# The first expert layer of a two-block network: activation halves side by side in one 512-column matmul, added after the bank is full

## The chip, the cores and the metric

The kernel runs on one core of one Trainium2 chip. The metric is the device time of one launch in microseconds. Five engines work side by side, each through its own list of instructions in a fixed order: TensorE (PE) multiplies matrices into PSUM, VectorE (DVE) and ScalarE (ACT) do the elementwise work, GpSimd (POOL) does almost nothing here, and SyncE (SP) issues the DMAs. An instruction that waits holds up everything behind it on its engine.

## The reference, cut to what matters

256 tokens of width 1024 pass through a first block (a recurrent and an attention branch, a gated feed-forward layer) and then through two layers of a second block. Each layer of the second block ends in a layer of 16384 small experts, which the reference computes only for the chosen ones:

```python
q = (xt @ w_q).reshape(T, PEER_HEADS, 2, PEER_HALF)
s = jnp.einsum('thpe,pne->thpn', q, sub_keys)
top_s, top_i = lax.top_k(s, PEER_TOPK)          # 16 of 128, for two key halves of 8 heads
...
best_s, best_j = lax.top_k(cand, PEER_TOPK)     # 16 of the 256 pairs
expert = idx_a * PEER_N_KEYS + idx_b
gate = jax.nn.softmax(best_s, axis=-1)
...
h = jnp.einsum('td,thkd->thk', xb, u[eb])
a = jax.nn.gelu(h, approximate=False) * gb
return jnp.einsum('thk,thkd->td', a, v[eb])
```

The kernel computes `h` for all experts (256 tokens by 16384 experts), multiplies by a gate matrix that is zero where an expert was not chosen, and multiplies by all of `v`. The result is the same sum.

## The kernel before

**Split products.** Every float32 operand of a large product is split in two parts in the rounded type F32R: `hi` is the rounded value (a cast on ACT, L225) and `lo` the rest (a subtraction on DVE, L226). A product is then three matmuls: high weight by high activation, high weight by low activation, low weight by high activation (`mm3`, L264 to L266; `step_a`, L281 to L283).

**Weights.** `weight` loads a tile of 128 by 2048 values by DMA and splits it in two halves of 1024 columns, so one half costs one `hi` cast and one `lo` subtraction. There are four buffers of split halves (`WBUFS`): the cast of a half waits until the TensorE is done with the half four places earlier. The preparation is put ahead in the program's priorities by 350 instructions (`AHEAD`).

**Expert layer (`peer`, run twice).** The first product works on pairs: `u_pair(j)` takes one weight tile, two blocks of 128 experts by 256 tokens. `proj_b` computes both blocks into one PSUM bank of 512 columns (256 for each block, tag `st`, two banks). Each of the 8 slices of 128 input values takes three matmuls of 256 columns, so a block is 24 matmuls and a pair 48. One Gelu on ACT (L1228) reads the bank and writes the ring `H`, which holds 40 pairs.

**Stages of an expert layer.** (1) Query products and scores; then DVE starts on `top16` (MAX8, FIND_INDEX8, MATCH_REPLACE8), the choice of the experts. (2) 24 pairs of `u` on TensorE, beside which DVE finishes the choice (`select`, `pick`, `gate`, `lookup`; the list `todo`), and `turn` transposes its results. (3) 16 further pairs of `u`, each with about one `gates` step, in which DVE builds one-hot matrices (L1239 to L1242), TensorE multiplies them (L1249, L1250) and DVE multiplies the gates into `H` (L1257). (4) 24 pairs of `u` in turn with `v_pair`, which multiplies `H` by a tile of `v` in 24 matmuls of 512 columns. (5) The rest of `v`.

**Order.** A list scheduler sets the order of each engine's instructions once, when the program is built, from the program's order and the priorities. The chip keeps to it.

Of the kernel before, what the change touches and what calls it, by code (L numbers as in the profile page):

```python
# [10 lines left out]
F32R = mybir.dt.float32r  # L11
F16 = mybir.dt.float16
U32 = mybir.dt.uint32
AF = mybir.ActivationFunctionType
ALU = mybir.AluOpType
# [3 lines left out]
S, D = 256, 1024  # L19
# [7 lines left out]
ALPHA = 4.0 ** 0.25  # L27
G_SCALE = 2048.0

PARTS = (48, 48, 32)  # second keys of the experts that are gated together  # L30
RING = 80  # second keys whose hidden values are on chip at a time
RATE = 0.96  # groups of 16 tokens gated for each tile of expert weights
AHEAD = 350  # instructions by which the weights' preparation runs ahead
WBUFS = 4  # split halves of weight tiles on chip
LEAD = 2  # tiles of the first block left when its attention is through
PACE = 2  # tiles of expert weights to a step of the selection
TURN = 17  # the tile after which the first half's indices are transposed
# memory keys and values of a layer, computed where norms leave the tensor engine free
FILL = ((), ("k1",), ("v1",), (), ("k0", "v0"))
URGENT = 1500  # instructions by which norms go before other work  # L40


def _btiles(w, cols):
# [121 lines left out]
def urgent(f):  # L165
    def run(self, *a, **k):
        with self.tc.high_priority(offset=URGENT):
            return f(self, *a, **k)
# [3 lines left out]
class Net:  # L172
    def __init__(self, ctx, tc, io, out):
# [3 lines left out]
        self.cp = pool("consts", 1)  # L177
        self.wp = pool("weights", WBUFS)
        self.xp = pool("state", 1)
# [36 lines left out]
    def vecs(self, *aps):  # L216
        with self.tc.high_priority(offset=AHEAD):
            t = self.wp.tile([128, 2048], F32, name="raw", tag="raw", bufs=3)
            out = [t[:, j * D:j * D + D] for j in range(len(aps))]
            for o, ap in zip(out, aps):  # L220
                self.nc.sync.dma_start(o, bass.AP(tensor=ap.tensor, offset=ap.offset, ap=[[0, 128], [1, D]]))
        return out
# [11 lines left out]
    def weight(self, src, parts=2):  # L234
        n = src.shape[-1] // parts
        out = []
        with self.tc.high_priority(offset=AHEAD):
            raw = self.raw(src)
# [5 lines left out]
        return out  # L244

    def new_xT(self, nk=8):
        hi = self.xp.tile([128, 8, S], F32R, name="xTh", tag="xTh")
        lo = self.xp.tile([128, 8, S], F32R, name="xTl", tag="xTl")
        return hi, lo

    def to_T(self, dst, src, tt, nk=8, k0=0):
        nc = self.nc
# [15 lines left out]
    def proj_b(self, w, xT, m=128):  # L268
        ps = self.st()
        for n, (hi, lo) in enumerate(w):  # L270
            hi, lo = (t.rearrange("p (k c) -> p k c", c=m) for t in (hi, lo))
            nk = hi.shape[1]
            for k in range(nk):
                self.mm3(ps[:m, n * 256:(n + 1) * 256], hi[:, k], lo[:, k], xT[0][:, k, :], xT[1][:, k, :],
                         k == 0, k == nk - 1)
        return ps

    def step_a(self, ps, w, c, xT, k, t, first, last):
        mm = self.nc.tensor.matmul
        xh, xl = xT[0][:, k, t], xT[1][:, k, t]  # L280
        mm(ps, xh, w[0][:, c], start=first, stop=False)  # L281
        mm(ps, xh, w[1][:, c], start=False, stop=False)  # L282
        mm(ps, xl, w[0][:, c], start=False, stop=last)  # L283
# [47 lines left out]
        return self.sp.tile([128, n], F32, name=name, tag=f"{name}{n}")  # L331

    def table(self, func):
        """Has the table of func loaded behind the scalar engine's work so far."""
        t = self.col("warm")
        self.tc.keep_in_program_order(self.nc.scalar.activation(t, self.eps6, func))

# [56 lines left out]
    def layer_norm(self, acc, gb, xT=None, out=None):  # L394
# [3 lines left out]
        for tt in range(2):  # L398
# [14 lines left out]
            for nh in range(2):  # L413
# [6 lines left out]
                    nc.sync.dma_start(out[tt * 128:tt * 128 + 128, c], x[:, c])  # L420
                if xT is not None:
                    self.to_T(xT, x[:, c], tt, nk=4, k0=4 * nh)
# [1 line left out]
    def load_mem(self):  # L424
        self.memT = tuple(self.mp.tile([128, 8, S], F32R, name=f"memT{s}") for s in "hl")
        raw = self.raw(self.io["memT"].rearrange("p k t -> p (k t)")).rearrange("p (k t) -> p k t", k=8)
        self.split(*self.memT, raw)
        self.km = [self.kp.tile([128, 2, S], F32, name=f"km{l}") for l in range(2)]
        self.vm = [self.kp.tile([128, 2, S], F32, name=f"vm{l}") for l in range(2)]
# [118 lines left out]
    def first_mix(self):  # L548
# [176 lines left out]
        for n, (name, j, f) in enumerate(tiles):  # L725
            f(j, self.proj_b(self.weight(io[name][j]), xT))
            while done < len(units) and done * (len(tiles) - LEAD) < (n + 1) * len(units):
                unit(*units[done])
# [90 lines left out]
    def ple_gate(self, acc, bv, xT):  # L819
        nc = self.nc  # L820
        for tt in range(2):
            h = self.vp.tile([128, D], F32, name="hn", tag="hn")
            for nh in range(2):
# [3 lines left out]
                nc.vector.tensor_mul(h[:, c], h[:, c], self.pproj[:, tt, c])  # L827
                nc.vector.tensor_add(self.x[:, tt, c], self.x[:, tt, c], h[:, c])
                self.to_T(xT, self.x[:, tt, c], tt, nk=4, k0=4 * nh)
# [1 line left out]
    def mem_attn(self, qm, km, vm):  # L831
        nc, pp = self.nc, self.pp
        mP = {}
# [266 lines left out]
    def peer(self, l, xT):  # L1100
        nc, io, pp = self.nc, self.io, self.pp
        two = lambda ps: ps.rearrange("p (a b) -> p a b", a=2)
# [4 lines left out]
        idx = [pp.tile([128, S], F16, name=f"pidx{j}") for j in range(4)]  # L1107
        H = pp.tile([128, RING, S], F32, name="H")
        tk = ExitStack()
# [113 lines left out]
        latest = [None]  # L1223

        def u_pair(j):
            ps = self.proj_b(self.weight(io["u"][l][j]), xT)
            s = (2 * j) % RING
            latest[0] = nc.scalar.activation(H[:, s:s + 2, :], two(ps), AF.Gelu)  # L1228

        def gates(part, t0):  # L1230
            b0, nb = sum(PARTS[:part]), PARTS[part]
            oa = op.tile([128, 4, P_KEYS, 4], F16, name="oa", tag="oa", bufs=2)
            ob, oh, ol = (op.tile([128, 4, max(PARTS), 4], F16, name=n, tag=n, bufs=k)[:, :, :nb]
                          for n, k in (("ob", 1), ("oh", 2), ("ol", 2)))
            c = slice(t0, t0 + 16)
            col = lambda j, n: idx[j][:, c].rearrange("p (g t) -> p g t", t=4)[:, :, None, :].to_broadcast(
                [128, 4, n, 4])
            iot = lambda n0, n: iota[:, None, n0:n0 + n, :].to_broadcast([128, 4, n, 4])
            nc.vector.tensor_tensor(out=oa, in0=iot(0, P_KEYS), in1=col(0, P_KEYS), op=ALU.is_equal)  # L1239
            nc.vector.tensor_tensor(out=ob, in0=iot(b0, nb), in1=col(1, nb), op=ALU.is_equal)  # L1240
            nc.vector.tensor_tensor(out=oh, in0=ob, in1=col(2, nb), op=ALU.mult)
            nc.vector.tensor_tensor(out=ol, in0=ob, in1=col(3, nb), op=ALU.mult)  # L1242
            nt = 16 if nb <= 32 else 8
            for e in range(16 // nt):
                ps = self.ms()
                for n in range(nt):
                    t = e * nt + n
                    o = ps[:, n * nb:n * nb + nb]
                    nc.tensor.matmul(o, oa[:, t // 4, :, t % 4], oh[:, t // 4, :, t % 4], start=True, stop=False)  # L1249
                    nc.tensor.matmul(o, oa[:, t // 4, :, t % 4], ol[:, t // 4, :, t % 4], start=False, stop=True)  # L1250
                g = ps[:, :nt * nb].rearrange("p (t b) -> p b t", t=nt)
                done = 0
                while done < nb:
                    s = (b0 + done) % RING
                    n = min(nb - done, RING - s)
                    h = H[:, s:s + n, t0 + e * nt:t0 + e * nt + nt]
                    nc.vector.scalar_tensor_tensor(h, g[:, done:done + n], 1.0 / G_SCALE, h, op0=ALU.mult,  # L1257
                                                   op1=ALU.mult)
                    done += n
# [3 lines left out]
        def v_prep(j):  # L1263
            s = (2 * j) % RING
            ah = op.tile([128, 2, S], F32R, name="ah", tag="ah", bufs=2)
# [33 lines left out]
        for tt in range(2):  # L1299
            todo += [lambda tt=tt: pick(tt, 0, 4), lambda tt=tt: pick(tt, 4, 4), lambda tt=tt: gate(tt),  # L1300
                     lambda tt=tt: lookup(tt)]
        n0 = PARTS[0] // 2
        for j in range(n0):
            u_pair(j)
            while todo and (10 - len(todo)) * PACE <= j:
                todo.pop(0)()
            if j == TURN:
                turn(0)
# [5 lines left out]
        op = ok.enter_context(self.tc.tile_pool(reuse_waits="tile", name="onehot", bufs=1))  # L1314
        ends = [sum(PARTS[:k + 1]) // 2 for k in range(len(PARTS))]
        queue = [(k, t0) for k in range(len(PARTS)) for t0 in range(0, S, 16)]
        up, vp, due, turn_v = n0, 0, 0.0, True
        while vp < 62:
            low = ends[queue[0][0] - 1] if queue and queue[0][0] else (0 if queue else 64)
            can_u = up < 64 and 2 * up + 2 <= 2 * vp + RING  # L1320
            can_v = vp < low
# [4 lines left out]
            elif can_u:  # L1326
                u_pair(up)
                up += 1
                turn_v = True
            due = min(due + RATE, 2.0) if queue else 0.0  # L1330
            while queue and up >= ends[queue[0][0]] and (due > 0.99 or not (can_u or can_v)):
# [84 lines left out]
```

## Time and profile before

| | |
|---|---|
| time, median of 3 runs (lowest, highest) | 2532.6 us (2531.86, 2533.39) |
| span of the profiled execution | 2531.2 us |
| PE busy | 2497.7 us, 99% |
| DVE busy | 1733.8 us, 68% |
| ACT busy | 1194.2 us, 47% |
| TensorE clock granted, mean | 0.994 of full speed |

The span runs from the first to the last instruction of one profiled execution; the times of the runs hold what lies around it too, here 1.4 us at the median. The first expert layer begins at about 700 us of the span, the second at about 1700 us. A busy TensorE is one with a matmul in flight, so the distance between the starts of two matmuls tells more of its rate than the duration of one.

### The profile page before, as it was taken

To read this page: it belongs to the slowest core of one execution; us is meant where nothing else is said; L and a number is where in the kernel's file an instruction comes from. 1 tells how busy PE (TensorE), PEld (TensorE's weight loads), DVE (VectorE), ACT (ScalarE), POOL (GpSimd) and SP (SyncE) were. 2 spreads that over 40 slices of the span, in tenths; PEclk is the share of its full clock that TensorE was granted. 3 is DMA by queue.
4 is the path that set the end of the run, shared out by engine and by line. 5 is a ranking of instruction groups with operands and counts; after the bars stand their busy time and mean duration, and the time that the engine had idled before them with its cause. 6 is when DMAs were issued, how large, how long until landed. Compare 5 with 4: busy or idle time off the path is not lost.

```text
span 2531.2 us, 44590 instructions
## 1 busy us (share of the span) xinstructions
PE 2497.7 (99%) x18560; PEld 2276.9 (90%) x18560; DVE 1733.8 (68%) x3195; ACT 1194.2 (47%) x1697; POOL 5.9 (0%) x17
## 2 busy tenths in 40 slices
PE   8999999999999999999999999999999999999998
PEld 7998899988799999999988888989999999998887
DVE  5357665565699587588478556669968758748756
ACT  5357554455545533433443445644643443344443
POOL 0000000000000000000000000000000000000000
PEclk9989999999999999999999999999999999999999
DMA  8422455543444544544544554344553454454454
GB/s 295 150 96 92 140 209 190 183 173 109 154 170 167 195 142 148 191 157 143 191 167 156 194 195 158 140 175 165 183 179 139 161 189 143 158 183 167 166 187 147
DMA packets 64410, 420.80 MB, mean 166 GB/s; under 512 B 7520, under 2 KB 10480, under 8 KB 15824
## 3 DMA queue, kind: packets, MB, share of 16 engines
q1 hardware_dynamic: 64208, 417.96, 47.4%
q8 instruction: 145, 2.38, 0.4%
q14 instruction: 57, 0.47, 0.1%
HBM read 416.88 MB, written 1.05 MB: 165 GB/s over the span
## 4 chain that ended last, share of the span: by engine, by line
PE 94%; DVE 3%; ACT 1%; DMA 1%; issue 1%; SPq 0%; DVEq 0%; ACTq 0%
PE ps_st L264 15%; PE ps_st L266 15%; PE ps_st L265 15%; PE ps_acc L281 12%; PE ps_acc L283 12%; PE ps_acc L282 12%; PE ps_ms L1249 3%; PE ps_ms L1250 3%; PE ps_sc L621 1%; PE ps_acc L640 1%; DVE lo L226 1%; ACT hi L225 1%; PE ps_acc L1152 1%; PE ps_sc L494 1%; PE ps_ms L1053 0%
## 5 line engine op out<-in xcount | busy, mean ns | idle before, releaser
L226 DVE TENSOR_TENSOR lo<-raw,hi 128x1024 fp32r<-128x1024 f32 (+1 forms) x762 | 922.8, 1214 | 508.5 <-ACT hi L225 505.5
L225 ACT CAST hi<-raw 128x1024 fp32r<-128x1024 f32 (+1 forms) x762 | 792.8, 1043 | 939.7 <-PE ps_st L265 610.1
L264 PE MATMUL ps_st<-xTh,hi 128*128 128x256 f32 (+1 forms) x3232 | 924.0, 286 | 0.9 <-DVE shift_v L573 0.7
L266 PE MATMUL ps_st<-xTh,lo 128*128 128x256 f32 (+1 forms) x3232 | 919.0, 284 | 0.5 <-DVE lo L226 0.5
L265 PE MATMUL ps_st<-xTl,hi 128*128 128x256 f32 (+1 forms) x3232 | 918.3, 284 | 0.0
L264 PEld LDWEIGHTS ps_st<-xTh,hi 128*128 128x128 f32 (+1 forms) x3232 | 619.3, 192 | 5.6 <-issue 2.0
L265 PEld LDWEIGHTS ps_st<-xTl,hi 128*128 128x128 f32 (+1 forms) x3232 | 618.8, 191 | 4.2 <-issue 1.4
L266 PEld LDWEIGHTS ps_st<-xTh,lo 128*128 128x128 f32 (+1 forms) x3232 | 618.4, 191 | 4.5 <-issue 2.7
L281 PE MATMUL ps_acc<-hi,ah 128*128 128x512 f32 x1024 | 403.8, 394 | 0.0
L282 PE MATMUL ps_acc<-lo,ah 128*128 128x512 f32 x1024 | 399.0, 390 | 0.0
L283 PE MATMUL ps_acc<-hi,al 128*128 128x512 f32 x1024 | 398.2, 390 | 0.0
L283 PEld LDWEIGHTS ps_acc<-hi,al 128*128 128x128 f32 x1024 | 192.1, 188 | 40.9
L281 PEld LDWEIGHTS ps_acc<-hi,ah 128*128 128x128 f32 x1024 | 192.9, 188 | 37.5
L282 PEld LDWEIGHTS ps_acc<-lo,ah 128*128 128x128 f32 x1024 | 192.6, 188 | 37.4
L225 ACT CAST ah<-H 128x512 fp32r<-128x512 f32 x128 | 79.5, 623 | 178.4 <-PE ps_acc L282 178.4
L226 DVE TENSOR_TENSOR al<-H,ah 128x512 fp32r<-128x512 f32 x128 | 88.4, 692 | 86.3 <-ACT ah L225 86.3
L1249 PE MATMUL ps_ms<-oh,oa 128*128 128x48 f16 (+1 forms) x1536 | 144.3, 214 | 0.0
L1249 PEld LDWEIGHTS <-oa 128*128 128x128 f16 x1536 | 131.1, 117 | 14.0 <-DVE lo L226 10.5
L1250 PE MATMUL ps_ms<-ol,oa 128*128 128x48 f16 (+1 forms) x1536 | 143.0, 214 | 0.0
L1250 PEld LDWEIGHTS <-oa 128*128 128x128 f16 x1536 | 133.9, 118 | 0.0
L1257 DVE SCALAR_TENSOR_TENSOR H<-ps_ms,H 128x256 f32<-128x256 f32 (+2 forms) x224 | 96.6, 457 | 40.7 <-PE ps_ms L1250 40.5
L1239 DVE TENSOR_TENSOR oa<-iota,pidx 128x2048 f16<-128x2048 f16 x96 | 116.7, 1215 | 0.0
(365 smaller groups left out, 2234.5 us busy)
## 6 DMA issues: line engine op xcount, KB each, us to landing
raw<-in_u SPq DMA_DIRECT2D x128, 1024.0 KB, 4.8
raw<-in_v SPq DMA_DIRECT2D x128, 1024.0 KB, 4.8
raw<-in_w_gu SPq DMA_DIRECT2D x22, 1024.0 KB, 4.8
raw<-in_w_pq SPq DMA_DIRECT2D x16, 1024.0 KB, 4.9
raw<-in_w_out SPq DMA_DIRECT2D x12, 1024.0 KB, 4.9
raw<-in_w_down SPq DMA_DIRECT2D x11, 1024.0 KB, 4.8
raw<-in_b_q SPq DMA_DIRECT2D x9, 1024.0 KB, 4.8
raw<-in_a_vr SPq DMA_DIRECT2D x6, 1024.0 KB, 4.9
```

The lines of the kernel that those rows point to most:

```text
L225: self.nc.scalar.copy(hi, src)
L226: self.nc.vector.tensor_sub(lo, src, hi.bitcast(F32))
L264: mm(ps, wh, xh, start=first, stop=False)
L265: mm(ps, wh, xl, start=False, stop=False)
L266: mm(ps, wl, xh, start=False, stop=last)
L281: mm(ps, xh, w[0][:, c], start=first, stop=False)
L282: mm(ps, xh, w[1][:, c], start=False, stop=False)
L283: mm(ps, xl, w[0][:, c], start=False, stop=last)
L1239: nc.vector.tensor_tensor(out=oa, in0=iot(0, P_KEYS), in1=col(0, P_KEYS), op=ALU.is_equal)
L1249: nc.tensor.matmul(o, oa[:, t // 4, :, t % 4], oh[:, t // 4, :, t % 4], start=True, stop=False)
L1250: nc.tensor.matmul(o, oa[:, t // 4, :, t % 4], ol[:, t // 4, :, t % 4], start=False, stop=True)
L1257: nc.vector.scalar_tensor_tensor(h, g[:, done:done + n], 1.0 / G_SCALE, h, op0=ALU.mult, op1=ALU.mult)
```

## The change

`u_pair` no longer uses `proj_b`. The new `proj_w` gives each block of 128 experts a bank of its own. The high and low halves of the activations now lie side by side in one tile, so that for each of the 8 slices the high weight meets both in one matmul of 512 columns; the low weight meets the high half in one of 256 columns, added to the bank's first half. The bank then holds two partial sums of 256 columns each. ACT copies the second to `H`, DVE adds the first to it, and after both blocks one Gelu runs on `H` in place. `proj_b` stays for all other products. Comments were dropped too.

```diff
     def new_xT(self, nk=8):
-        hi = self.xp.tile([128, 8, S], F32R, name="xTh", tag="xTh")
-        lo = self.xp.tile([128, 8, S], F32R, name="xTl", tag="xTl")
-        return hi, lo
+        x = self.xp.tile([128, 8, 2, S], F32R, name="xT", tag="xT")
+        return x[:, :, 0], x[:, :, 1], x
...
+    def proj_w(self, w, xT):
+
+        out = []
+        mm = self.nc.tensor.matmul
+        for hi, lo in w:
+            ps = self.st()
+            hi, lo = (t.rearrange("p (k c) -> p k c", c=128) for t in (hi, lo))
+            for k in range(8):
+                mm(ps, hi[:, k], xT[2][:, k].rearrange("p s t -> p (s t)"), start=k == 0, stop=False)
+                mm(ps[:, :S], lo[:, k], xT[0][:, k, :], start=False, stop=k == 7)
+            out.append(ps)
+        return out
...
         def u_pair(j):
-            ps = self.proj_b(self.weight(io["u"][l][j]), xT)
             s = (2 * j) % RING
-            latest[0] = nc.scalar.activation(H[:, s:s + 2, :], two(ps), AF.Gelu)
+            for n, ps in enumerate(self.proj_w(self.weight(io["u"][l][j]), xT)):
+                nc.scalar.copy(H[:, s + n, :], ps[:, S:])
+                nc.vector.tensor_tensor(out=H[:, s + n, :], in0=H[:, s + n, :], in1=ps[:, :S], op=ALU.add)
+            latest[0] = nc.scalar.activation(H[:, s:s + 2, :], H[:, s:s + 2, :], AF.Gelu)
```

In the changed kernel most lines of `peer` stand 12 lower: L1240 is the copy, L1241 the addition, L1242 the Gelu, L1127 to L1132 the instructions of `top16` and L1191 the exponential of `gate` (L1179 before).

DVE in stage 2 of the first expert layer, before: `lo` is a weight half, MAX, MAX_INDEX and MATCH_REPLACE belong to the choice.

```order
L1118 MATCH_REPLACE rest<-ts_6678,ps_acc 128x128
L1115 MAX ts_6678<-ps_acc 128x8
L1119 MAX ts_6678<-rest 128x8
L1116 MAX_INDEX ti_6680<-ts_6678,ps_acc 128x8
L1120 MAX_INDEX ti_6680<-ts_6678,rest 128x8
L1118 MATCH_REPLACE rest<-ts_6678,ps_acc 128x128
L226 TENSOR_TENSOR lo<-raw,hi 128x1024
L1119 MAX ts_6678<-rest 128x8
L1165 TENSOR_TENSOR cand<-ts_6677 128x4x16
```

The same place now; `H<-H,ps_st` is the addition that gives a bank back.

```order
L1127 MAX ts_6671<-ps_acc 128x8
L226 TENSOR_TENSOR lo<-raw,hi 128x1024
L1241 TENSOR_TENSOR H<-H,ps_st 128x256
L1131 MAX ts_6671<-rest 128x8
L1128 MAX_INDEX ti_6673<-ts_6671,ps_acc 128x8
L1132 MAX_INDEX ti_6673<-ts_6671,rest 128x8
L226 TENSOR_TENSOR lo<-raw,hi 128x1024
L1241 TENSOR_TENSOR H<-H,ps_st 128x256
L1130 MATCH_REPLACE rest<-ts_6671,ps_acc 128x128
L1177 TENSOR_TENSOR cand<-ts_6670 128x4x16
```

Each block's addition stands right behind the `lo` of the block four places later, and between two such pairs stand instructions of the choice.

ACT near the end of stage 2, before, around the exponential of the second half of the tokens; the waits in brackets name the engines or DMA queues.

```order
L225 CAST hi<-raw 128x1024 [waits DMAHW0_49,DVE_49,PE_49]
L225 CAST hi<-raw 128x1024 [waits DVE_49,PE_49]
L1228 ACTIVATE H<-ps_st 128x512 [waits PE_49]
L1179 ACT_TABLE_LOAD
L1179 ACTIVATE pgate<-pgate 128x128
L225 CAST hi<-raw 128x1024 [waits DMAHW1_49,DVE_49,PE_49]
L225 CAST hi<-raw 128x1024 [waits DVE_49,PE_49]
L1228 ACT_TABLE_LOAD
L1228 ACTIVATE H<-ps_st 128x512 [waits PE_49]
```

The same place now.

```order
L1242 ACTIVATE H<-H 128x512 [waits DVE_49]
L225 CAST hi<-raw 128x1024 [waits DMAHW0_49,PE_49,Activation_49]
L1240 COPY H<-ps_st 128x256 [waits PE_49]
L225 CAST hi<-raw 128x1024 [waits PE_49,Activation_49]
L1240 COPY H<-ps_st 128x256 [waits PE_49]
L1242 ACTIVATE H<-H 128x512 [waits DVE_49]
L225 CAST hi<-raw 128x1024 [waits DMAHW1_49,PE_49,Activation_49]
L1191 ACT_TABLE_LOAD
L1191 ACTIVATE pgate<-pgate 128x128
L225 CAST hi<-raw 128x1024 [waits PE_49,Activation_49]
L1240 COPY H<-ps_st 128x256
L1240 COPY H<-ps_st 128x256 [waits PE_49]
```

A Gelu waited for TensorE before and waits for DVE now; a copy stands behind each cast, and the table load and the exponential stand between two casts of one tile.

TensorE in the changed kernel, from the last matmuls of the second block on: the third block's first matmul waits.

```order
L285 MATMUL ps_st<-xT,hi 128x512
L286 MATMUL ps_st<-xT,lo 128x256
L1164 MATMUL ps_acc<-sub,pq 128x128 [waits DVE_49]
L1164 MATMUL ps_acc<-sub,pq 128x128 x3
L285 MATMUL ps_st<-xT,hi 128x512 [waits DVE_49,Activation_49]
L286 MATMUL ps_st<-xT,lo 128x256
```

From here on the first matmul of each block has such a wait for DVE, where before only the first of a pair could have one for ACT.

## Rows read from the trace of the kernel before

**Rows 1.** The page, part 1: busy time and share of the engines.

```profile
PE 2497.7 (99%) x18560; PEld 2276.9 (90%) x18560; DVE 1733.8 (68%) x3195; ACT 1194.2 (47%) x1697; POOL 5.9 (0%) x17
```

**Rows 2.** The page, part 4: shares of the chain that ended last, by engine.

```profile
PE 94%; DVE 3%; ACT 1%; DMA 1%; issue 1%; SPq 0%; DVEq 0%; ACTq 0%
```

**Rows 3.** Windows: start, end, length; busy us of PE, PEld, DVE, ACT, POOL; clock, DMA.

```profile
700.00:800.00 100.00, 100.00 (x841) 100.00 (x840) 95.76 (x426) 49.81 (x56) 0.00 (x0) 1.00 0.46 159
1100.00:1200.00 100.00, 100.00 (x924) 91.66 (x923) 87.06 (x143) 36.69 (x42) 0.00 (x0) 1.00 0.43 147
1700.00:1800.00 100.00, 100.00 (x841) 100.00 (x840) 95.81 (x427) 49.09 (x55) 0.00 (x0) 1.00 0.48 160
```

**Rows 4.** Timeline of PE in stage 4: start, duration, instruction; first matmuls of three runs.

```profile
1008.50 0.28 PE L264 MATMUL ps_st<-xTh,hi 128*128 128x256 f32 x1
...
1014.26 0.40 PE L281 MATMUL ps_acc<-hi,ah 128*128 128x512 f32 x1
...
1019.73 0.28 PE L264 MATMUL ps_st<-xTh,hi 128*128 128x256 f32 x1
```

**Rows 5.** Timeline of PE where stage 2 of the first layer begins.

```profile
734.05 0.36 PE L264 MATMUL ps_st<-xTh,hi 128*128 128x256 f32 x1
...
739.88 1.05 PE L1152 MATMUL ps_acc<-sub,pq 128*128 128x128 f32 x8
740.69 0.36 PE L264 MATMUL ps_st<-xTh,hi 128*128 128x256 f32 x1
```

**Rows 6.** Timeline of DVE through the choice of the experts, first layer.

```profile
705.99 0.30 DVE L1115 MAX8 ts<-ps_acc 128x8 f32<-128x128 f32 x1 [1.58 <-PE ps_acc L1152]
...
745.24 1.22 DVE L226 TENSOR_TENSOR lo<-raw,hi 128x1024 fp32r<-128x1024 f32 x1
746.37 0.29 DVE L1119 MAX8 ts<-rest 128x8 f32<-128x128 f32 x1
...
747.36 0.28 DVE L1118 MATCH_REPLACE8 rest<-ts,ps_acc 128x128 f32<-128x128 f32 x1
747.56 0.29 DVE L1115 MAX8 ts<-ps_acc 128x8 f32<-128x128 f32 x1
...
825.87 0.40 DVE L1214 TENSOR_TENSOR cols<-ex 128x128 f32<-128x128 f16 x1
```

**Rows 7.** Groups by line and shape: busy us, mean ns | idle before.

```profile
L790 DVE TENSOR_TENSOR glu<-glu,ps_st 128x256 f32<-128x256 f32 x20 | 8.3, 413 | 0.0
...
L789 ACT ACTIVATE glu<-ps_st 128x256 f32<-128x256 f32 x20 | 7.6, 379 | 0.0
```

**Rows 8.** Timeline of ACT late in stage 2: idle time before an instruction in brackets.

```profile
850.71 1.05 ACT L225 CAST hi<-raw 128x1024 fp32r<-128x1024 f32 x1 [1.83 <-PE ps_st L265]
851.66 0.60 ACT L1228 ACTIVATE H<-ps_st 128x512 f32<-128x512 f32 x1
853.59 1.05 ACT L225 CAST hi<-raw 128x1024 fp32r<-128x1024 f32 x1 [1.33 <-PE ps_st L265]
```

**Rows 9.** Timeline of DVE at the same place.

```profile
851.79 1.23 DVE L226 TENSOR_TENSOR lo<-raw,hi 128x1024 fp32r<-128x1024 f32 x1 [1.65 <-ACT hi L225]
```

**Rows 10.** Timeline of ACT: the second exponential of the choice.

```profile
834.57 1.28 ACT L1179 ACT_TABLE_LOAD   x1
835.87 0.31 ACT L1179 ACTIVATE pgate<-pgate 128x128 f32<-128x128 f32 x1
```

**Rows 11.** Timeline of ACT: Gelus of stage 3, the first and the twelfth.

```profile
908.70 0.60 ACT L1228 ACTIVATE H<-ps_st 128x512 f32<-128x512 f32 x1
...
989.47 0.60 ACT L1228 ACTIVATE H<-ps_st 128x512 f32<-128x512 f32 x1
```

**Rows 12.** Windows at the program's end, columns as in rows 3.

```profile
2523.00:2524.00 1.00, 0.24 (x2) 0.00 (x0) 1.00 (x2) 0.00 (x0) 0.00 (x0) 1.00 0.94 350
2526.00:2527.00 1.00, 0.00 (x0) 0.00 (x0) 1.00 (x3) 0.00 (x0) 0.00 (x0) 0.92 0.00 0
2527.00:2528.00 1.00, 0.00 (x0) 0.00 (x0) 1.00 (x2) 0.00 (x0) 0.00 (x0) 0.50 0.00 0
```

## The prediction

> **What bounds the kernel now.** I read the page's shares first: TensorE (PE) is busy for 99% of the span [rows 1] and carries 94% of the chain that ended last [rows 2]. So time is saved where TensorE gets less to do, and lost where it is made to wait. The windows then show the room beside it: while the experts are chosen, DVE is busy for 95.8 of 100 us in either layer, and for 87.1 where `u` and `v` alternate, with TensorE never idle in any of them [rows 3]. A DVE that is full costs nothing today because TensorE asks it for only one thing in those stages, the `lo` halves of the weights, and these run up to three blocks ahead.
>
> **What the matmuls save.** The timeline gives both rates from starts. 48 matmuls of 256 columns take 1014.26 - 1008.50 = 5.76 us, 0.120 each; 24 of 512 columns take 1019.73 - 1014.26 = 5.47 us, 0.228 each [rows 4]. A pair costs 48 x 0.120 = 5.76 us now. It will be 16 x 0.228 + 16 x 0.120 = 5.57 us, 2.78 for a block, so 0.19 us less. Over 128 pairs that is 24.6 us if TensorE never waits. The streamed columns are the same; what goes is the fixed part of 16 matmuls, 0.240 - 0.228 = 0.012 us each. The Trainium skill, "TensorE: Matmul & The Clock Gate", section "Back-to-back issue gap", gives a stream's step as N/2.4 + 2.5 ns, so a fixed part of 2.5 ns: by it a pair would save 0.04 us and the change 5 us. The trace has 0.120 and 0.228 us where that formula has 0.109 and 0.216, so it does not agree, and the sum goes by the rows.
>
> **What the evacuation adds.** Each block gets one copy on ACT (nearest row: 128x256 from PSUM, 379 ns) and one addition on DVE (nearest: 128x256 with one PSUM operand, 413 ns) [rows 7]. DVE instructions overlap a little: the 1.22 us `lo` at 745.24 is followed at 746.37, after 1.13 [rows 6], so an addition takes 0.33 us of the queue. The Gelu stays, with the same 128x512 shape. New is a wait: `st` has two banks, a block now takes one, and so block n+2 cannot start before the addition of block n is through. TensorE had 5.76 us for one Gelu; it has one block, 2.78 us, for a copy, an addition and all that stands ahead of them on two engines. Behind the waiting matmul stands all of TensorE's work.
>
> **Stage 2, blocks 1 to 31 (DVE sets the pace).** Only the order tells what stands ahead of an addition. Counting through DVE's rows of the changed kernel from the first MAX8 on: ahead of the first addition stand 118 instructions of the choice and 11 `lo`. In the kernel before, the same 118 and 12 `lo` were through at 747.56 [rows 6]. So the first addition ends at about 747.56 - 1.13 + 0.41 = 746.8. Block 1 starts at 734.05 [rows 5]; block 3 could start at 734.05 + 2 x 2.78 + 0.81 for the scores = 740.4 and waits 6.4 us.
>
> It goes on so. Ahead of addition 30 stand 300 instructions of the choice, 39 `lo` and 29 additions. Before, the same 300 with 38 `lo` were through at 825.87 [rows 6]. One more `lo` and 30 additions make 825.87 + 1.13 + 30 x 0.33 = 836.9, and block 32 starts then. Before, block 3 started at 740.69 [rows 5] and block 32 at 740.69 + 29 x 2.88 = 824.2. That is 12.7 us late. It assumes a DVE that waits no more than before. But after every second block the Gelu on ACT now waits for an addition, the next cast stands behind the Gelu (0.5 us) and takes 1.05, and DVE has the next `lo` about 1.6 us after that addition: where less of the choice stands in between, DVE waits. Walking the 30 blocks by hand with these durations I find some five such places and three at the copies of `ex`, 0.2 to 0.7 us each, about 1.8 us beyond what DVE already waited. Late by 14.5 us; bounds 11 (no gaps, additions of 0.28) and 18 (every such place twice as long).
>
> **Blocks 32 to 48 (a ring of latencies).** The choice is over, DVE has room. Let a block end at 0. The cast for the block four places on starts at 0.1 and takes 1.05, `lo` starts 0.03 after it [rows 8, 9] at 1.18 and holds DVE for 1.13, the addition ends at 2.31 + 0.41 = 2.72, and the bank is needed at 2.78: just in time. For the block after a Gelu the cast starts 0.4 later, and TensorE waits 0.4. That makes the next pair's chain catch up, so it falls on every second pair: 5.57 + 0.2 = 5.77 a pair, against 5.76. No gain here; bounds -0.2 and +0.3 us a pair, for 8 pairs. Once in this stretch, the table load and the exponential (1.28 + 0.2 us [rows 10]) stand between two casts, and this block's addition stands behind the second `lo`: cast to 1.5 because of the Gelu, table and exponential to 2.9, cast to 4.0, `lo` to 5.1, addition to 5.6, so TensorE waits 2.9 us. Before, this was hidden by the weights' lead. Stage 2 is 17.4 us longer in each layer.
>
> **Stage 3.** A pair with its gate step takes (989.47 - 908.70)/11 = 7.34 us now [rows 11], of which 7.34 - 5.76 = 1.58 are gate matmuls. These stand between pairs and give the additions that much more time; in the steady order (addition, gates into `H`, one-hot, `lo`, addition, one-hot, gates into `H`, `lo`) I find no wait. Ten of the 16 pairs are in it: -1.9 us. The first six stand mostly back to back as in the ring above: 0.
>
> **Stage 4.** 5.5 us of `v` stand between pairs, so banks are free in time. DVE's 87.1 of 100 us [rows 3] become about 87.1 + 14 x 0.33 = 91.7 of 98.7, 93% (a pair with its `v` and two gate steps takes 5.76 + 5.47 + 2 x 1.58 = 14.4 us, so 7 pairs, 14 additions). I count the saving in full: 24 x 0.19 = -4.6 us.
>
> **Hidden at no cost.** ACT's copies (256 x 0.3 us) have room at 50% busy [rows 3], apart from the ring above. The activations in one tile change the strides of `to_T` only; outside the expert layers the orders differ in a few rows, and SP's and POOL's not at all, so DMAs start in the same sequence: 0, bounds -1 and +1.
>
> **Sum.** In each layer 14.5 + 2.9 - 1.9 - 4.6 = 10.9; both have the same order and the same load [rows 3]: 21.8. The profiled span of 2531.2 becomes 2553.0; with the 1.4 us that the runs' median holds beyond it, 2554.4. The bounds of the first term alone give 2547 to 2561, with the ring's bounds 2544 to 2566.
>
> **Rivals.**
> *The banks come free in time* (faster). If the additions were through within a block's 2.78 us, TensorE would keep all of the saving: 2532.6 - 24.6 = 2508. This needs a DVE that reaches the addition early; the full windows of rows 3 and the order, with the first addition at 746.8 and not before 740.4, speak against it. What remains open is how late: the change breaks even at 6.5 us of delay per layer in stage 2, where I have 17.4. A quicker addition alone, at 0.2 us, takes off only 4.
> *DVE is the bound in stage 4 too* (slower still). At 93%, with waits of its own in that queue, it may pass delays to TensorE, which also needs one-hot matrices and emptied gate banks from it. The 24 pairs with their `v` and gates are some 340 us a layer; 1 to 2% of it gives 3.4 to 7, so 2561 to 2568. Against it: at 87% TensorE waited for nothing [rows 3].
> *The clock falls in the waits* (slower). After its last matmul TensorE stood idle from 2523 on, and its granted clock went from 1.00 to 0.92 and then 0.50, that is from 2.4 to 1.2 GHz, in the windows at 2526 and 2527 [rows 12]. The wait at block 3 is longer than that. At the lower clock block 3 takes up to 2.8 us more, but its addition stands behind 22 more instructions of the choice, so most of it is hidden; a fall at the exponential would not be. 0 to 3 us a layer, up to 2560. The Trainium skill, same page, section "Why this matters for your kernels", asks for no idle gaps between bursts of matmuls, since the clock falls in them; this end of the program agrees.
> *The mixed widths save nothing* (slower). Rows 4 show each width only in runs of its own. If a 512 followed by a 256 takes as long as three of 256, the 13 us of stages 3 and 4 go too: 2567. Against it: the step from 256 to 512 and back at 1014.26 and 1019.73 shows no extra time [rows 4]. The Trainium skill's formula above lies between, at about 2564.
>
> **How the numbers follow.** A run of this kernel can be told from another at about 0.2%, 5 us. Chances: my forecast 0.64 (own range 2544 to 2566), banks in time or a delay so short that it breaks even 0.14, stage 4 bound 0.14, clock 0.06, no saving 0.02. The second holds all that is faster and most of what is the same, half each; of the forecast's lower tail 0.03 lies within 5 us of before. Faster 0.07, same 0.10, slower 0.83. The range leaves out the fast end and the worst of stage 4: 2536 to 2570.
>
> **What the profile will show.** Right: matmul starts 0.228 and 0.120 us apart in a block; TensorE idle some 6 us before the third block of each expert layer, and again by 0.3 to 2 us before most blocks up to the 31st, with the addition as releaser; block 32 at about 838 us; DVE busy for all of that stretch; a wait of 3 us at the exponential; stage 4 shorter by 0.19 a pair. Wrong: TensorE busy without a gap from 734 to 837, additions well under 0.33 us apart from their neighbours, or waits in stages 3 and 4 as large as in stage 2.

## The result and the profile after

The changed kernel takes 2563.7 us (median of four runs, 2563.1 to 2564.3) against 2532.4 for the kernel before (2531.9 to 2533.4): ratio 1.0123, 95% interval 1.0110 to 1.0137. It is slower by 31 us. The span grows from 2531.2 to 2561.3 us, by 30.1 where 21.8 had been worked out.

The page's parts 1 and 4 of the changed kernel, for [rows 1] and [rows 2]:

```profile
PE 2500.9 (98%) x16512; PEld 2167.7 (85%) x16512; DVE 1819.6 (71%) x3451; ACT 1275.1 (50%) x1953; POOL 5.9 (0%) x17
...
PE 87%; DVE 9%; ACT 2%; issue 1%; DMA 1%; DVEq 0%; SPq 0%; ACTq 0%
```

DVE's part of the chain has grown from 3% to 9%: it now ends waits of TensorE. The windows of [rows 3], now, say where:

```profile
700.00:800.00 100.00, 92.71 (x601) 82.85 (x599) 94.81 (x420) 46.46 (x64) 0.00 (x0) 0.97 0.42 148
1100.00:1200.00 100.00, 100.00 (x816) 85.13 (x815) 89.81 (x155) 41.22 (x56) 0.00 (x0) 1.00 0.42 148
1700.00:1800.00 100.00, 92.84 (x619) 84.11 (x617) 89.29 (x388) 46.49 (x63) 0.00 (x0) 0.97 0.48 169
```

In the first and the last TensorE (first busy column) is idle for 7 us and its clock is 0.97; in the middle one, stage 4, it has no gap and the clock is full. What it waited for, from the waits of PE (total us, times, longest):

```profile
PE ps_st L285 <- DVE H L1241: 19.9, 15, 6.2
...
PE ps_st L285 <- DVE cols L1199: 5.9, 2, 3.0
```

The first matmul of a block waits for the addition (L1241). The second row is the same wait at the exponential: L1199 ended just behind the addition there (856.93 against 856.79 in the first layer), and the waiting is put down to it.

The timeline shows the first wait on PE, and the order on DVE that makes it:

```profile
739.36 1.05 PE L1164 MATMUL ps_acc<-sub,pq 128*128 128x128 f32 x8
746.65 0.77 PE L285 MATMUL ps_st<-xT,hi 128*128 128x512 f32 x1 [6.24 <-DVE H L1241]
```
```profile
745.87 0.31 DVE L1130 MATCH_REPLACE8 rest<-ts,ps_acc 128x128 f32<-128x128 f32 x1
746.06 0.44 DVE L1241 TENSOR_TENSOR H<-H,ps_st 128x256 f32<-128x256 f32 x1
746.39 0.32 DVE L1131 MAX8 ts<-rest 128x8 f32<-128x128 f32 x1
746.60 0.43 DVE L1241 TENSOR_TENSOR H<-H,ps_st 128x256 f32<-128x256 f32 x1
```

Block 1's addition stands in a DVE that has no gap around it, as in [rows 6]. It starts at 746.06, and block 3 follows at 746.65.

How late the changed kernel is at a place, in the first layer (starts of matmuls, after less before; "reckoned" adds up the prediction's terms):

| place | before | after | late by | reckoned |
|---|---|---|---|---|
| block 32 | 824.28 | 839.16 | 14.9 | 14.5 |
| block 49, stage 3 begins | 874.03 | 894.44 | 20.4 | 17.4 |
| block 83, second pair of stage 4 | 1008.50 | 1025.76 | 17.3 | about 15.3 |
| block 127, last pair | 1281.06 | 1296.32 | 15.3 | about 11.1 |
| a whole layer | 999.29 | 1014.76 | 15.5 | 10.9 |

The last row is the time from the first MAX8 of one layer to that of the next (1705.28 less 705.99 before, 1720.42 less 705.66 after). Up to block 32 it came out as reckoned to 0.4 us. The missing 4.6 us are these 0.4, 2.6 between blocks 32 and 49, of which 1.0 comes back up to block 83, and 2.2 between blocks 83 and 127; the last 0.4 is mostly the first MAX8 itself, which comes 0.3 us earlier in the changed kernel.

### The profile page after: what moved, and what is told of

It reads as the page before. It is cut to its first block, busy times and chain, and to the rows that moved or that the text cites. A ratio compares the mean times of both kernels' runs of the same rounds, so it can differ in the third digit from the quotient of the medians.

```text
span 2561.3 us, 41063 instructions
## 1 busy us (share of the span) xinstructions
PE 2500.9 (98%) x16512; PEld 2167.7 (85%) x16512; DVE 1819.6 (71%) x3451; ACT 1275.1 (50%) x1953; POOL 5.9 (0%) x17
## 4 chain that ended last, share of the span: by engine, by line
PE 87%; DVE 9%; ACT 2%; issue 1%; DMA 1%; DVEq 0%; SPq 0%; ACTq 0%
PE ps_st L285 17%; PE ps_acc L293 12%; PE ps_acc L295 11%; PE ps_acc L294 11%; PE ps_st L286 8%; PE ps_st L265 5%; PE ps_st L264 5%; PE ps_st L263 5%; DVE lo L226 3%; PE ps_ms L1263 3%; PE ps_ms L1264 3%; ACT hi L225 1%; PE ps_sc L633 1%; PE ps_acc L652 1%; DVE rest L1130 1%
## 5 line engine op out<-in xcount | busy, mean ns | idle before, releaser
L285 PE MATMUL ps_st<-xT,hi 128*128 128x512 f32 x2048 | 743.1, 405 | 26.6 <-DVE H L1241 19.9
L286 PE MATMUL ps_st<-xT,lo 128*128 128x256 f32 x2048 | 577.8, 282 | 0.0
L285 PEld LDWEIGHTS ps_st<-xT,hi 128*128 128x128 f32 x2048 | 388.8, 190 | 129.9 <-DVE H L1241 20.4
L286 PEld LDWEIGHTS ps_st<-xT,lo 128*128 128x128 f32 x2048 | 390.2, 191 | 1.5
L263 PE MATMUL ps_st<-xT,hi 128*128 128x256 f32 (+1 forms) x1184 | 340.3, 287 | 0.9 <-DVE shift_v L585 0.7
L265 PE MATMUL ps_st<-xT,lo 128*128 128x256 f32 (+1 forms) x1184 | 339.4, 287 | 0.5 <-DVE lo L226 0.5
L264 PE MATMUL ps_st<-xT,hi 128*128 128x256 f32 (+1 forms) x1184 | 339.0, 286 | 0.0
L265 PEld LDWEIGHTS ps_st<-xT,lo 128*128 128x128 f32 (+1 forms) x1184 | 225.7, 191 | 4.5 <-issue 2.7
L263 PEld LDWEIGHTS ps_st<-xT,hi 128*128 128x128 f32 (+1 forms) x1184 | 225.8, 191 | 4.2 <-issue 2.0
L264 PEld LDWEIGHTS ps_st<-xT,hi 128*128 128x128 f32 (+1 forms) x1184 | 225.8, 191 | 2.9 <-issue 1.4
L1242 ACT ACTIVATE H<-H 128x512 f32<-128x512 f32 x128 | 80.9, 632 | 163.6 <-DVE H L1241 163.6
L1263 PEld LDWEIGHTS <-oa 128*128 128x128 f16 x1536 | 131.6, 118 | 19.6 <-DVE lo L226 8.9
```

The source lines that it names most:

```text
L263: mm(ps, wh, xh, start=first, stop=False)
L264: mm(ps, wh, xl, start=False, stop=False)
L265: mm(ps, wl, xh, start=False, stop=last)
L285: mm(ps, hi[:, k], xT[2][:, k].rearrange("p s t -> p (s t)"), start=k == 0, stop=False)
L286: mm(ps[:, :S], lo[:, k], xT[0][:, k, :], start=False, stop=k == 7)
L1242: latest[0] = nc.scalar.activation(H[:, s:s + 2, :], H[:, s:s + 2, :], AF.Gelu)
```

## The experiments

"A layer" below is that same time from MAX8 to MAX8, against the 999.29 us of before. It leaves out what the first block does, whose time moved by a few us between kernels. It holds the work between the two expert layers, and there the granted clock fell to 0.50 for some 3.3 us (between 1525 and 1544 us) in `prio`, `filler` and `late_grouped` and in no other of these kernels. From the first MAX8 to the start of block 127 these three stand at +4.2, +12.9 and -6.5, beside +15.6 for the changed kernel and -3.9 for `late`. The runs of before that were taken beside these eight have the medians 2532.4 and 2532.5.

| kernel | time, us | ratio to before (interval) | a layer |
|---|---|---|---|
| changed kernel | 2563.7 | 1.0123 (1.0110 to 1.0137) | +15.5 |
| late | 2525.2 | 0.9974 (0.9964 to 0.9983) | -3.5 |
| early | 2570.8 | 1.0156 (1.0139 to 1.0173) | +19.6 |
| six_banks | 2530.9 | 0.9991 (0.9981 to 1.0000) | -1.3 |
| no_add | 2527.0 | 0.9979 (0.9970 to 0.9989) | -3.3 |
| prio | 2541.8 | 1.0035 (1.0022 to 1.0047) | +5.1 |
| filler | 2559.0 | 1.0100 (1.0083 to 1.0116) | +13.2 |
| late_grouped | 2520.3 | 0.9950 (0.9933 to 0.9966) | -5.6 |
| mix | 2513.3 | 0.9922 (0.9905 to 0.9938) | -10.0 |

### late and early: each half of the change alone

```diff
 def u_pair(j):
     s = (2 * j) % RING
+    if j < 24:        # "early" has: if j >= 24
+        ps = self.proj_b(self.weight(io["u"][l][j]), xT)
+        latest[0] = nc.scalar.activation(H[:, s:s + 2, :], two(ps), AF.Gelu)
+        return
```

> Pairs 0 to 23 of each expert layer (stage 2) are computed as in the kernel before; pairs 24 to 63 (stages 3 and 4) as in the changed one. Theory 'place in DVE's queue' (the loss is all in stage 2, where additions stand behind the choice of the experts): stages 3 and 4 keep what the changed kernel's trace shows for them, about 0.11 us a pair, so 2532.4 - 80 x 0.11 = 2523.6, and no wait for an addition over 0.5 us. By the size that the prediction had for a pair (0.19): 2517. Rival 'DVE is too full everywhere' (the load itself is what is passed on): at 89% in stage 4 additions make TensorE late there too, 2532 or more.

> The other half: pairs 0 to 23 as in the changed kernel, pairs 24 to 63 as before. If the two halves add up, this one loses what stage 2 lost in the changed kernel, about 19.2 us a layer: 2532.4 + 38.4 = 2571, slower than the changed kernel itself. If the lateness of stage 2 is given back in stages 3 and 4 (a wait there that simply shortens), 2545 or less.

Measured: 2525.2 and 2570.8. The halves add up: -3.5 and +19.6 make +16.1 a layer, where the whole change has +15.5. (In this layer the granted clock fell to 0.50 once more in `early` than in the changed kernel, from 813 to 816 us.) Stages 3 and 4 gain, and all of the loss is in stage 2. The gain is what the changed trace had, not the 0.19 us a pair of the prediction. Gelus of stage 4 stand 11.22 us apart before and 11.10 in `late`:

```profile
1048.95 0.59 ACT L1228 ACTIVATE H<-ps_st 128x512 f32<-128x512 f32 x1
1060.17 0.59 ACT L1228 ACTIVATE H<-ps_st 128x512 f32<-128x512 f32 x1
```
```profile
1048.51 0.63 ACT L1246 ACTIVATE H<-H 128x512 f32<-128x512 f32 x1 [1.35 <-DVE H L1245]
1059.61 0.63 ACT L1246 ACTIVATE H<-H 128x512 f32<-128x512 f32 x1 [1.35 <-DVE H L1245]
```

The rival that DVE is the bound in stage 4 falls: from 1100 to 1200 TensorE has no gap while DVE is busy for 89.8 us, in the changed kernel and in `late`.

### six_banks: the same additions, more banks

```diff
-for n, ps in enumerate(self.proj_w(self.weight(io["u"][l][j]), xT)):
+for n, ps in enumerate(self.proj_w(self.weight(io["u"][l][j]), xT, "acc" if j < 24 and j % 3 else "st")):
```

(`proj_w` takes its bank from the pool with that name.)

> The changed kernel, but in stage 2 two of three pairs take their banks from the four of v's sums, which stand empty there, so a block may wait for an addition some six blocks back instead of two. Theory 'place in the queue': the first addition still ends near 747, but is wanted only at 751; no wait at block 3, no fall of the clock, and the 14 us of blocks 1 to 31 go with most of the wait at the exponential: 2563.7 - 2 x 17 = 2530 (2520 to 2538). Rival 'load': DVE was full and has got 10 us more work in this stretch, which TensorE has to wait for however many banks there are: 2550 or more.

Measured: 2530.9, 32.8 us less than the changed kernel, although the additions, the copies and the matmuls are the same. The windows from 760 to 860:

```profile
760.00:860.00 100.00, 100.00 (x578) 87.40 (x578) 95.74 (x295) 69.50 (x105) 0.00 (x0) 1.00 0.53 188
```

TensorE has no gap beside a DVE that is busy for 95.7 of 100 us. So the load of the additions is not what is paid, and the rival "load" falls. Block 3 no longer waits, it follows the scores at 743.01. But block 4 does, for another cause:

```profile
743.01 0.50 PE L285 MATMUL ps_acc<-xT,hi 128*128 128x512 f32 x1
...
750.01 0.79 PE L285 MATMUL ps_acc<-xT,hi 128*128 128x512 f32 x1 [3.91 <-DVE rest L1130]
750.60 0.41 PE L286 MATMUL ps_acc<-xT,lo 128*128 128x256 f32 x1
750.82 0.63 PE L285 MATMUL ps_acc<-xT,hi 128*128 128x512 f32 x1
```

The four banks are not all empty yet: the choice (L1130) still reads the last scores there. Behind the wait the matmuls run at half the clock (0.63 + 0.41 us where 0.40 + 0.28 is usual; the granted clock is 0.50 from 750 to 755). Counted from the first MAX8, block 5 starts 6.5 us later than before in the first layer and 5.3 in the second. So the number came out at 2530 partly by luck: without this wait it would be lower.

### no_add: the additions left out

```diff
 nc.scalar.copy(H[:, s + n, :], ps[:, S:])
-nc.vector.tensor_tensor(out=H[:, s + n, :], in0=H[:, s + n, :], in1=ps[:, :S], op=ALU.add)
```

> The changed kernel without its additions: the copy on ACT stays, but the half of the sum from the high activations is left out of H. Theory 'place in the queue': a bank then waits for ACT's copy only, and the matmuls' saving of about 0.11 us a pair shows in all 128 pairs: 2532.4 - 14 = 2518 (2514 to 2522). Rival 'ACT and the bank' (the copy behind the Gelu and the cast, or one bank to a block, is what costs): 2545 or more. Rival 'mixed widths' (the pairs themselves are no shorter): 2532.

Measured: 2527.0 (span 2523.7), 9 us more than expected. The loss goes with the addition, but of a layer's 7 us of saving only 3.3 are left. PE's waits name ACT, the other engine that empties a bank, and ACT's timeline tells why (four waits in the two layers, 3.7 us a layer, which is what is missing):

```profile
PE ps_st L285 <- ACT H L1240: 7.4, 4, 2.8
```
```profile
811.00 1.90 ACT L1218 COPY ex<-ij 128x2048 f16<-128x2048 f16 x1 [4.07 <-DVE ij L1210]
812.81 1.04 ACT L225 CAST hi<-raw 128x1024 fp32r<-128x1024 f32 x1
813.75 0.36 ACT L1240 COPY H<-ps_st 128x256 f32<-128x256 f32 x1
```

ACT stands for 4.07 us at the copy `ex` of the choice, which waits for DVE, and the block's copy stands two rows behind it. Half of the theory held; that a copy on the half-empty ACT costs nothing did not. In the changed kernel no wait of TensorE for a bank is put down to ACT: there the addition is later still.

### prio: the additions earlier in DVE's order

```diff
-nc.vector.tensor_tensor(out=H[:, s + n, :], in0=H[:, s + n, :], in1=ps[:, :S], op=ALU.add)
+with self.tc.high_priority(offset=AHEAD):
+    nc.vector.tensor_tensor(out=H[:, s + n, :], in0=H[:, s + n, :], in1=ps[:, :S], op=ALU.add)
```

> The changed kernel with the additions given the same lead in the order as the weights' halves have. In DVE's order the first addition then has 94 instructions of the choice ahead of it instead of 118, but the 30th still 290 instead of 300. If the work that stands ahead on DVE sets each block (as in the prediction's sum), the wait at block 3 is gone or under 1 us and the clock stays up there, yet block 32 is only 10 x 0.26 = 2.6 us earlier: 2563.7 - 2 x 2.6 = 2558 (2554 to 2562). Rival: what is lost is the long wait at block 3 and the fall of the clock behind it, some 6 to 9 us a layer: 2546 to 2552.

Measured: 2541.8, better than every expectation. I had priced the ten instructions of the choice that now stand behind addition 30 at a mean of 0.26 us. They are the long ones, and counted from the first MAX8 block 32 starts 8.6 us earlier than in the changed kernel, not 2.6. DVE of `prio` behind its 30th addition (first row):

```profile
830.87 0.41 DVE L1242 TENSOR_TENSOR H<-H,ps_st 128x256 f32<-128x256 f32 x1
831.20 1.22 DVE L1222 TENSOR_TENSOR ex<-ex,t 128x2048 f16<-128x2048 f16 x1
...
833.80 1.64 DVE L1225 TENSOR_TENSOR ex<-ex 128x1024 f16<-128x1024 f16 x3
...
840.74 1.23 DVE L1219 TENSOR_TENSOR ex<-ex,sel 128x2048 f16<-128x2048 f16 x1 [0.51 <-ACT ex L1218]
```

In the changed kernel the matching addition starts at 838.69, and the choice is nearly done by then. DVE waits from there on:

```profile
838.69 0.41 DVE L1241 TENSOR_TENSOR H<-H,ps_st 128x256 f32<-128x256 f32 x1
839.02 0.39 DVE L1226 TENSOR_TENSOR cols<-ex 128x128 f32<-128x128 f16 x1
840.74 1.22 DVE L226 TENSOR_TENSOR lo<-raw,hi 128x1024 fp32r<-128x1024 f32 x1 [1.33 <-ACT hi L225]
```

One comparison sums it up: windows of the changed kernel, then of `prio`, from 706.4 to 838 and from 838 to 892.

```profile
706.40:838.00 131.60, 121.32 (x737) 105.42 (x736) 128.55 (x511) 69.45 (x98) 0.00 (x0) 0.97 0.43 152
838.00:892.00 54.00, 51.05 (x288) 43.19 (x287) 33.21 (x51) 30.00 (x49) 0.00 (x0) 0.97 0.45 158
```
```profile
706.40:838.00 131.60, 126.64 (x785) 110.81 (x784) 129.49 (x512) 72.44 (x106) 0.00 (x0) 1.00 0.45 161
838.00:892.00 54.00, 52.89 (x312) 44.81 (x311) 39.26 (x59) 33.20 (x53) 0.00 (x0) 1.00 0.48 175
```

In the first stretch DVE is as full in both (128.6 and 129.5 us), but TensorE is busy for 5.3 us more in `prio`; DVE's other work is done later, in a stretch where it had 21 us to spare.

### filler: the waits stay, the clock does not fall

```diff
+wt = self.weight(io["u"][l][j])
+if j in (1, 18):
+    fl = self.acc() if j > 1 else self.ms()
+    for k in range(10 if j > 1 else 22):
+        nc.tensor.matmul(fl, wt[0][0][:, :128], xT[2][:, k % 8].rearrange("p s t -> p (s t)"), start=True, stop=True)
...
```

> The changed kernel with useless matmuls of 512 columns put into its two long waits, 22 ahead of block 3 and 10 ahead of block 37 of each layer (5.0 and 2.3 us), into banks that nobody reads. The waits stay, the clock should not fall. If the fall at block 3 is hidden by the additions that come late anyway, and only that at the exponential counts: blocks 5 to 31 start within 0.5 us of where they did, blocks from 38 on 1.5 us earlier, 2563.7 - 3 = 2560.5. Rival: both falls are paid in full, 2.1 + 1.6 us a layer: 2556. Rival: the clock costs nothing there: 2563.7.

Measured: 2559.0. Windows of the changed kernel, then of `filler`:

```profile
740.00:760.00 20.00, 13.74 (x67) 11.56 (x66) 19.17 (x100) 7.15 (x11) 0.00 (x0) 0.83 0.22 81
850.00:870.00 20.00, 17.08 (x89) 14.38 (x88) 9.89 (x19) 11.04 (x16) 0.00 (x0) 0.91 0.39 141
```
```profile
740.00:760.00 20.00, 17.78 (x96) 14.72 (x95) 19.73 (x102) 7.92 (x12) 0.00 (x0) 1.00 0.29 110
850.00:870.00 20.00, 19.41 (x107) 16.30 (x106) 11.46 (x20) 13.02 (x22) 0.00 (x0) 1.00 0.44 157
```

The clock stays at 1.00 (2.4 GHz), and a layer is 2.2 us shorter (1012.5 instead of 1014.8). That lies between the first two expectations: the fall at the exponential is paid in full, and that at block 3 is not wholly hidden. By the Gelus, and counted from each kernel's first MAX8, `filler` is 1.1 us ahead of the changed kernel at pair 16 (from 0) and 2.7 at pair 18. It is still 2.7 us ahead at block 127; behind that its clock falls once more, as said above.

### late_grouped: the widths one after the other

```diff
 for k in range(8):
     mm(ps, hi[:, k], xT[2][:, k].rearrange("p s t -> p (s t)"), start=k == 0, stop=False)
+for k in range(8):
     mm(ps[:, :S], lo[:, k], xT[0][:, k, :], start=False, stop=k == 7)
```

> As the run with only pairs 24 to 63 changed, but a block's eight matmuls of 512 columns stand first and its eight of 256 behind them. In the changed kernel 512 and 256 take turns and a turn takes 0.352 us where 0.228 + 0.120 = 0.348 was forecast, so a block 2.81 and not 2.78. If the change of width costs that, it now falls once in a block: 2.79, 0.05 to 0.07 us a pair, 80 pairs: 4 to 5.6 us less than that run, 2520 to 2521. Rival: it is a matter of the weights that each matmul needs anew, or of the 0.228 itself in this place: no change, 2525.

Measured: 2520.3, as forecast for the change of width. That is 2.1 us a layer less than `late`, and 2.6 up to block 127. In the changed kernel the widths take turns:

```profile
1083.76 0.40 PE L285 MATMUL ps_st<-xT,hi 128*128 128x512 f32 x1
1083.99 0.28 PE L286 MATMUL ps_st<-xT,lo 128*128 128x256 f32 x1
...
1085.16 0.40 PE L285 MATMUL ps_st<-xT,hi 128*128 128x512 f32 x1
```

Four turns take 1085.16 - 1083.76 = 1.40 us, 0.35 each, where the rates of [rows 4] add up to 0.348; by the starts of whole blocks it is 2.81 us a block, against 2.78. In `late_grouped` (eight of a kind in a row of the view):

```profile
1074.12 1.98 PE L285 MATMUL ps_st<-xT,hi 128*128 128x512 f32 x8
1075.93 1.12 PE L287 MATMUL ps_st<-xT,lo 128*128 128x256 f32 x8
...
1079.68 0.21 PE L1268 MATMUL ps_ms<-oh,oa 128*128 128x48 f16 x1
```

A pair takes 1079.68 - 1074.12 = 5.56 us, the 5.57 of the prediction to 0.01. So it is the taking of turns that costs; what in TensorE makes it so, no run here shows.

### mix: both lessons together

Pairs 0 to 2 go by the old path, pairs 3 to 23 by the banks of `six_banks`, the widths are grouped.

```diff
-    if j < 24:
+    if j < 3:
...
-    for n, ps in enumerate(self.proj_w(self.weight(io["u"][l][j]), xT)):
+    for n, ps in enumerate(self.proj_w(self.weight(io["u"][l][j]), xT, "acc" if j < 24 and j % 3 else "st")):
```

(shown against `late_grouped`)

> Pairs 0 to 2 of each layer as in the kernel before (while the last scores still hold their banks), pairs 3 to 23 changed with two of three pairs in the banks of v's sums, the rest changed, and in all of them the widths grouped. By the theory 'place in the queue' no addition is waited for over 1 us, and 61 pairs keep 0.15 to 0.19 us each less about 2 us at the changes of path and at the exponential: 2532.4 - 2 x (9.2 to 11.6 - 2) = 2513 to 2518. Rival 'load' (DVE's 10 us more in stage 2 come out somewhere, as late weights): 2525 or more.

Measured: 2513.3, faster than both kernels. Stage 2 in the first and the second layer:

```profile
740.00:860.00 120.00, 120.00 (x726) 107.24 (x725) 115.25 (x382) 80.54 (x116) 0.00 (x0) 1.00 0.52 188
1730.00:1850.00 120.00, 120.00 (x723) 107.12 (x722) 115.06 (x382) 81.12 (x117) 0.00 (x0) 1.00 0.52 186
```

TensorE has no gap although the additions are as late as ever. The first changed block, and its addition on DVE:

```profile
753.27 2.00 PE L285 MATMUL ps_st<-xT,hi 128*128 128x512 f32 x8
755.11 1.12 PE L287 MATMUL ps_st<-xT,lo 128*128 128x256 f32 x8
756.06 0.63 PE L285 MATMUL ps_st<-xT,hi 128*128 128x512 f32 x2
```
```profile
764.80 0.42 DVE L1246 TENSOR_TENSOR H<-H,ps_st 128x256 f32<-128x256 f32 x1
```

The block ends at 756.06 and its addition starts 8.7 us later. With two banks the block after the next would have waited 8.7 + 0.4 - 2.8 = 6.3 us for it; with six it did not wait.

The Trainium skill, "Perfetto Trace Analysis", section "Matmul Optimizations", advises to have all eight banks of PSUM in use. By it the four banks of the sums should not stand empty in stage 2; six_banks and mix agree (-32.8 us against the changed kernel, no gap in 120 us).

## Why the prediction was right, and where its sizes were off

**The sign and the main term.** Blocks 1 to 31 were to be paced by DVE and late by 14.5 us; block 32 came at 839.2 where 838 was said, 14.9 late, with the first wait 6.24 us (6.4 said) and the first addition through at 746.5 (746.8 said). Counting DVE's order and pricing it from rows was right. The closeness is in part luck: `filler` shows that 1.1 us of the 14.9 are the fall of the clock at block 3, which the sum had left out as mostly hidden. One sign did not come as said, the waits of 0.3 to 2 us "before most blocks": the profile has 13 waits beside the two of 6.2 us, in both layers together, and the rest of the delay stands in the distance of the blocks' starts, 3.19 us on the mean from block 3 to 32 ((839.16 - 746.65)/29) against 2.81. What the runs add is the cause: neither the additions' work nor their being late costs, but their being late with two banks. Given an earlier place (`prio`, -10.4 us a layer) more than half of the term goes: counted from the first MAX8, block 32 is 6.6 us late instead of 15.2. With more banks (`six_banks`, -16.7) it goes but for the wait at block 4, and in `mix` it is gone: block 32 is 2.2 us early there.

**The ring and the exponential, 2.9 us, were too small.** From block 32 to 49 the kernel lost 5.5 us. The wait at the exponential is 2.92 us and 3.0 in the waits above, as said. Then block 37 ran at half the clock:

```profile
856.94 0.58 PE L285 MATMUL ps_st<-xT,hi 128*128 128x512 f32 x1 [2.92 <-DVE cols L1199]
857.32 0.41 PE L286 MATMUL ps_st<-xT,lo 128*128 128x256 f32 x1
857.53 0.63 PE L285 MATMUL ps_st<-xT,hi 128*128 128x512 f32 x1
```

It lasted 861.37 - 856.94 = 4.4 us instead of 2.8. This is the rival "the clock falls in the waits", of 0 to 3 us a layer, and it came in beside the forecast: by `filler` 2.7 us in the first layer, 1.1 of it at block 3 and 1.6 here. So the sum put at nothing a cost that it had named as a rival. The rest of the 2.6 is no waiting: 27 gate matmuls stand ahead of block 49 now, and none before. Windows of the matmuls that read `oa` (first column with a count is PE), from block 32 to 49, before and now:

```profile
824.28:874.03 49.75, 0.00 (x0) 0.00 (x0) 0.94 (x1) 1.00 0.58 204
```
```profile
839.16:894.44 55.28, 1.44 (x27) 1.30 (x27) 2.44 (x2) 0.97 0.48 169
```

By the starts of the matmuls around them they take 1.3 us (16 behind block 44, 11 behind block 48). The ring itself came out as said: without them, two blocks from block 41 on take 5.73 to 5.77 us, where 5.77 was worked out.

**Stage 4, -4.6 us, was too large.** The step that failed is "It will be 16 x 0.228 + 16 x 0.120 = 5.57 us": both rates are right in runs of one width, but not where widths take turns. A pair gained 0.11 us instead of 0.19, and stage 4 gave back 2.0 to 2.6 instead of 4.6. That is the rival "the mixed widths save nothing" come true in part: some 0.08 of 0.19 us is lost to the turns, and grouping brings the forecast 5.57 back.

**Stage 3, -1.9 us.** Between blocks 49 and 83 the kernel won 3.1 us, but 1.3 of it are the gate matmuls that were already done. `early`, whose pairs go by the old path there, has the same 27 matmuls ahead of block 49 and wins 1.3 us in the six pairs behind it. The other 1.8 us are some 0.11 a pair in every pair, where the sum had 0.19 in ten pairs and nothing in six: the size of this term came out by luck.

**The other rivals.** *Banks in time* did not happen, but `mix` shows its time nearly: 2513, where 2508 was worked out for all 128 pairs. *DVE the bound in stage 4* fell with `late`. The layout costs what was said, nothing within 1 us: the span of `late` is 2523.5, 7.7 us under before, and its two layers account for 2 x 3.5 = 7.0.

## What to carry to other kernels

When an edit gives an accumulator's emptying to an engine that is already full, do not ask how long the new instruction takes, but where it stands in that engine's order and how many buffers bridge the time until its turn: here 0.33 us of work cost up to 6 us a block with two banks and nothing with six. Before looking for a better place on that engine, look for buffers that stand empty in that stage. And read a pitch from rows of the very sequence you plan: two widths in turns ran slower than the sum of their own rates, and grouping them restored it.

## What was not expected of the hardware

Matmuls of 512 and 256 columns in turns take 0.35 us a couple, where runs of each take 0.228 and 0.120 [rows 4]; eight and eight give 2.78 us a block instead of 2.81. The granted clock fell to 0.50 (1.2 GHz) right behind a wait of 2.92 us (block 37) as well as within one of 6.24 us (block 3), and the block behind took 4.4 and 5.0 us instead of 2.8 (block 3 runs from 746.65 to 751.66); useless matmuls in the waits kept it at 1.00. Windows of the changed kernel in the wait at block 3 and in block 37, columns as in [rows 3]:

```profile
745.00:746.00 1.00, 0.00 (x0) 0.00 (x0) 1.00 (x8) 0.00 (x0) 0.00 (x0) 0.50 1.01 426
...
858.00:859.00 1.00, 1.00 (x5) 0.90 (x4) 0.00 (x0) 0.00 (x0) 0.00 (x0) 0.50 0.84 336
```
